# A matmul with scale and add on one core: five hand-written engine programs with their own semaphores in place of a framework's order, and a loop on TensorE

## The chip, the core and the metric

The kernel runs on one core of one Trainium2 chip. The core has five engines that run side by side, each with its own list of instructions: TensorE (PE in the profile; its weight loads are listed as PEld), VectorE (DVE), ScalarE (ACT), GpSimd (POOL) and SyncE (SP), which here only issues transfers. Sixteen DMA engines move data between the chip's memory and the core's on-chip memory. The metric is the time on the device in microseconds (us); smaller is better.

## The reference

```python
batch, m, k, n = 16, 512, 1024, 768
x: (16, 512, 1024) float32     weight: (1024, 768) float32
scale: 0.1                     add_value: (16, 512, 768) float32

return (scale * np.matmul(x, weight) + add_value).astype(np.float32)
```

Taken together the batches give 8192 rows of x. The kernel cuts them into 64 tiles of 128 rows. Each tile is a product of 128 x 1024 by 1024 x 768, and to its result, scaled, 128 x 768 values are added. All in all 33.55 MB of x, 3.15 MB of weight and 25.17 MB of add_value are read, and 25.17 MB are written.

## The kernel before

**Transfers.** `STREAM` lists every transfer in the order in which SP issues them: "x" loads tiles of x, "w" loads slices of the weight, "a" loads add_value and "o" stores results; the two numbers are the first tile (or slice) and how many. All go through one queue. x has room for 16 tiles (`xs`), add_value and the results share 32 tiles' room (`ao`), and the weight lands in the last 8 places of `ao` before it is cast to bf16 (`w_bf`). A load of x waits until the tiles that it overwrites have been read; a store waits until its tiles have been finished; a load of add_value into used room waits until the store from that room has landed. Since SP is in order, what stands behind a waiting transfer waits with it.

**Turning x.** The product needs x with its 1024 inner values on the partitions, so each tile is turned. There are two ways. Tiles 0 to 13 are cast to bf16 (`cast_to`), turned by TensorE in four transposes against an identity matrix (`transpose`, L149), and copied out of PSUM by ACT or DVE (L157). Tiles 14 to 63 go in pairs (`MOVED`): ACT and POOL copy them to bf16 by quadrants of 32 partitions, four copies each for each half of the pair, eight copies each in all (`move_pair`, L110), and DVE turns the pair in one instruction, within 32 x 32 blocks (`turn_moved`, L119). The moved pairs have three buffers (`va`), the turned pairs three (`xt`).

**Products.** For each tile TensorE makes 16 matmuls, eight slices of the inner dimension by two parts of the columns (512 and 256), into one of three PSUM buffers `mm` (`product`, L170). Each weight load is an instruction of its own in the program. DVE then computes scale times the product plus add_value in place in `ao` (`finish`, L178). The first three tiles are multiplied slice by slice as the weight arrives (`head`), scaled into spare room, and their add_value is added later (`added`, L237). The last tile is finished in two parts, 512 columns and then 256.

**Order.** The author writes one sequence of instructions: `STREAM` drives it, `step` does one tile. In `step` the products of tile t come first, then its finish, then the turn of the pair that starts at t+4; the copies for pairs up to six tiles ahead stand in the middle of it. The Tile framework splits the sequence by engine and puts in the semaphores. Everything is unrolled: TensorE's program alone has 1024 products, 1024 weight loads and 56 transposes, 2,084 instructions with its waits.

Of the kernel before, what the change touches and what calls it, by code (L numbers as in the profile page):

```python
# [8 lines left out]

STREAM = [
    ("x", 0, 3), ("w", 0, 2), ("w", 2, 2), ("x", 3, 1), ("w", 4, 4), ("a", 0, 8),
    ("x", 4, 4), ("x", 8, 8), ("a", 8, 8), ("x", 16, 8), ("a", 16, 8), ("x", 24, 8),
# [5 lines left out]
X_SLOTS = 16  # L20
A_SLOTS = 32
XB_BUFS = 3
AHEAD = 4
EARLY = 3

MOVED = [14, 16, 18, 20, 22, 24, 26, 28, 30, 32, 34, 36, 38, 40, 42, 44, 46, 48, 50, 52, 54, 56, 58, 60, 62]
# [3 lines left out]
def kernel(  # L32
# [9 lines left out]
    P = 128  # L42
# [9 lines left out]

    KC = K // (2 * P)
    KJ = 2 * KC
    CUT = 512
    G = 8
# [3 lines left out]
    out_v = out_f.rearrange("(g p t) n -> p g t n", p=P, t=G)  # L60

    def rows(view, s, n):
# [3 lines left out]

    w_v = weight.rearrange("(c p r) n -> p c (r n)", p=P, r=2)

    const = ctx.enter_context(tc.tile_pool(name="const", bufs=1))
    xb_pool = ctx.enter_context(tc.tile_pool(name="xb_pool", bufs=XB_BUFS))  # L70
    xt_pool = ctx.enter_context(tc.tile_pool(name="xt_pool", bufs=3))
    va_pool = ctx.enter_context(tc.tile_pool(name="va_pool", bufs=3))
    tp_pool = ctx.enter_context(
        tc.tile_pool(name="tp_pool", bufs=2, space=bass.MemoryType.PSUM))
    mm_pool = ctx.enter_context(
        tc.tile_pool(name="mm_pool", bufs=3, space=bass.MemoryType.PSUM))
    ctx.enter_context(tc.manual_schedule())

    identity = const.tile([P, P], fp32, name="identity")
    make_identity(nc, identity)  # L80
    xs = const.tile([P, X_SLOTS, K], fp32, name="xs")
    ao = const.tile([P, A_SLOTS, N], fp32, name="ao")
    w_bf = const.tile([P, KJ, N], bf16, name="w_bf")

    xb_tiles, xt_tiles, mm_tiles, done = {}, {}, {}, {"cast": 0, "step": 0, "x": 0}
    in_pair = {t0 + i: t0 for t0 in MOVED for i in range(2)}
    moved, cast_pairs = {}, set()

    def load_w(j, n):

        s = A_SLOTS - KJ + j
        assert j % 2 == n % 2 == 0
        nc.sync.dma_start(  # L93
            ao[:, s:s + n, :].rearrange("p (c r) n -> p c (r n)", r=2),
            w_v[:, j // 2:(j + n) // 2, :])
        for i in range(n):
            nc.vector.tensor_copy(w_bf[:, j + i, :], ao[:, s + i, :])  # L97

    def move_pair(t0, half):


        if half == 0:
            va = va_pool.tile([P, 2 * KC, 4, 64], bf16, tag="va")
            moved[t0] = va
        k = t0 % X_SLOTS
        assert k + 1 < X_SLOTS
        src = xs[:, k:k + 2, :].rearrange("p i (c b k) -> p (i c) b k", b=4, k=64)
        for b in range(4):
            for a, move in ((2 * half, nc.scalar.copy), (2 * half + 1, nc.gpsimd.tensor_copy)):
                move(moved[t0][32 * b:32 * b + 32, :, a, :],  # L110
                     src[32 * a:32 * a + 32, :, b, :])
        if half == 1:
            cast_pairs.add(t0)

    def turn_moved(t0):
        xt = xt_pool.tile([P, 2, KC, P], fp32, tag="xt")
        for i in range(2):
            xt_tiles[t0 + i] = xt[:, i, :, :]
        nc.vector.transpose(  # L119
            xt.rearrange("p i c m -> p (i c m)"),  # L120
            moved.pop(t0).bitcast(fp32).rearrange("p c a k -> p (c a k)"))

    def cast_to(t):
        while done["cast"] <= t:
            i = done["cast"]
            if i in in_pair:
                assert in_pair[i] in cast_pairs
                done["cast"] += 1
                continue
            if len(xb_tiles) == XB_BUFS:  # L130
                break
# [168 lines left out]
```

## Time and profile before

The median of three runs was 210.06 us (209.99 to 210.46). The profiled execution spans 208.4 us from its first to its last instruction; a timed run has some 1.6 us more around that.

| what | busy, us (share) | instructions |
|---|---|---|
| 16 DMA engines, data, mean share | 97.9% | 4448 packets, 87.03 MB |
| PE | 177.1 (85%) | 1059 |
| POOL | 135.2 (65%) | 219 |
| ACT | 129.9 (62%) | 210 |
| DVE | 104.1 (50%) | 113 |
| profiled execution: span | 208.4 | 2843 |

The share of a DMA engine is the time that its packets took. A row of a group of instructions gives the source line, the engine, the operation, what it writes and reads, the shape, the count, the busy time and the mean of one in nanoseconds. "PEclk" is the granted TensorE clock, 1.00 being full speed. The DMA engines fetch the engines' instructions as well; those packets stand in queues of their own, marked "instruction".

### The profile page before, as it was taken

The page shows a single profiled execution, that of the slowest core. Times are in us where ns is not written, and L with a number is a line of the kernel's source. Part 1 is how long each engine was busy: PE and PEld are TensorE (multiplying, and loading weights), DVE is VectorE, ACT ScalarE, POOL GpSimd, SP SyncE. Part 2 cuts the span into 40 slices and gives each one's busy share as a digit, 9 for nine tenths or more (in the row PEclk, how much of TensorE's full clock was granted, in tenths as well). Part 3 has the DMA queues.
Part 4 walks back from the last instruction along what each step waited for, and adds up shares of the span by engine and source line. Part 5 has one row for each costly group of instructions (what it writes and reads, how often), then busy time and mean ns, then how long its engine had stood idle before and what let it go on. Part 6 is the DMA issues. An engine that isn't in the chain of part 4 may idle for free.

```text
span 208.4 us, 2843 instructions
## 1 busy us (share of the span) xinstructions
PE 177.1 (85%) x1059; PEld 108.4 (52%) x1080; DVE 104.1 (50%) x113; ACT 129.9 (62%) x210; POOL 135.2 (65%) x219
## 2 busy tenths in 40 slices
PE   0498339999999999999999999999959996799930
PEld 0355125666666666666666666666626563456510
DVE  0514713555675555566666645475054651555620
ACT  2421100540299999997999559992899919996000
POOL 1310051428699999999999759993899939997000
PEclk9999958999999999999999999999999999999995
DMA  6999999999999999999999999999999999999994
GB/s 229 413 440 448 420 459 406 440 453 415 402 464 434 413 415 425 458 415 428 415 439 451 407 436 425 450 428 407 439 426 437 453 404 426 434 437 425 423 414 187
DMA packets 4461, 87.21 MB, mean 418 GB/s; under 512 B 480, under 2 KB 480, under 8 KB 1120
## 3 DMA queue, kind: packets, MB, share of 16 engines
q1 hardware_dynamic: 4448, 87.03, 97.9%
q8 instruction: 8, 0.13, 0.2%
q14 instruction: 5, 0.04, 0.0%
HBM read 61.87 MB, written 25.17 MB: 418 GB/s over the span
## 4 chain that ended last, share of the span: by engine, by line
DMA 44%; PE 38%; POOL 10%; SPq 1%; issue 1%; DVE 1%; POOLq 0%; DVEq 0%
PE mm L170 36%; DMA out_dram<-ao 17%; DMA ao<-in_add_value_dram 15%; DMA xs<-in_x_dram 12%; POOL va L110 9%; PE tp L149 2%; DVE ao L178 1%; SPq L93 1%; SPq L250 1%; POOL xb L139 1%; SPq L256 0%; POOLq L139 0%; DVEq L178 0%
## 5 line engine op out<-in xcount | busy, mean ns | idle before, releaser
L170 PE MATMUL mm<-w_bf,xt 128*128 128x512 bf16 (+1 forms) x1003 | 170.6, 327 | 8.3 <-DVE ao L178 6.0
L110 ACT CAST va<-xs 32x512 bf16<-32x512 f32 x200 | 123.2, 616 | 46.0 <-DMA xs<-in_x_dram 43.5
L170 PEld LDWEIGHTS <-xt 128*128 128x128 bf16 x1024 | 101.0, 99 | 74.8 <-issue 5.5
L110 POOL CAST va<-xs 32x512 bf16<-32x512 f32 x200 | 121.7, 608 | 20.8 <-DMA xs<-in_x_dram 11.9
L178 DVE SCALAR_TENSOR_TENSOR ao<-mm,ao 128x768 f32<-128x768 f32 (+2 forms) x62 | 57.2, 935 | 40.3 <-PE mm L170 34.0
L119 DVE STREAM_TRANSPOSE xt<-va 128x1024 f32<-128x1024 f32 x25 | 31.1, 1244 | 29.5 <-POOL va L110 29.0
L139 POOL CAST xb<-xs 128x1024 bf16<-128x1024 f32 x11 | 11.2, 1043 | 29.4 <-DMA xs<-in_x_dram 21.8
L149 PE MATMUL tp<-identity,xb 128*128 128x128 f32 x56 | 10.2, 317 | 14.5 <-DVE xb L135 7.7
L149 PEld LDWEIGHTS tp<-identity,xb 128*128 128x128 f32 x56 | 7.7, 163 | 16.4 <-issue 7.7
L157 DVE COPY xt<-tp 128x1024 bf16<-128x1024 bf16 x10 | 6.9, 688 | 10.8 <-PE tp L149 10.8
L157 ACT COPY xt<-tp 128x512 bf16<-128x512 bf16 (+1 forms) x7 | 4.1, 655 | 9.2 <-PE tp L149 9.2
L97 DVE CAST w_bf<-ao 128x768 bf16<-128x768 f32 x8 | 4.0, 555 | 4.9 <-DMA ao<-in_weight_dram 4.9
L135 DVE CAST xb<-xs 128x512 bf16<-128x512 f32 x3 | 1.9, 695 | 7.1 <-DMA xs<-in_x_dram 7.1
L137 POOL CAST xb<-xs 128x512 bf16<-128x512 f32 x2 | 1.6, 835 | 5.9 <-DMA xs<-in_x_dram 5.9
L137 ACT CAST xb<-xs 128x512 bf16<-128x512 f32 x1 | 0.6, 619 | 5.1 <-DMA xs<-in_x_dram 5.1
L237 DVE TENSOR_TENSOR ao<-ao 128x768 f32<-128x768 f32 x3 | 2.7, 953 | 1.1 <-DMA ao<-in_add_value_dram 1.1
L206 DVE TENSOR_SCALAR ao<-mm 128x768 f32<-128x768 f32 x2 | 1.8, 953 | 2.5 <-PE mm L170 2.5
L137 ACT ACT_TABLE_LOAD x1 | 1.3, 1283 | 0.7 <-PEq L281 0.7
L203 ACT ACTIVATE ao<-mm 128x768 f32<-128x768 f32 x1 | 0.8, 817 | 0.0
masks.py:197 POOL MEMSET identity<- 128x128 f32 x1 | 0.2, 205 | 0.3 <-POOLq L281 0.3
masks.py:199 POOL TENSOR_SCALAR_AFFINE_SELECT identity<-identity 128x128 f32<-128x128 f32 x1 | 0.3, 293 | 0.1
L281 POOL MEMSET const-float32-0.0<- 128x1 f32 x1 | 0.1, 98 | 0.2 <-issue 0.2
(3 smaller groups left out, 0.3 us busy)
## 6 DMA issues: line engine op xcount, KB each, us to landing
xs<-in_x_dram SPq DMA_DIRECT2D x7, 4096.0 KB, 23.9
ao<-in_add_value_dram SPq DMA_DIRECT2D x8, 3072.0 KB, 31.1
out_dram<-ao SPq DMA_DIRECT2D x7, 3072.0 KB, 31.3
xs<-in_x_dram SPq DMA_DIRECT2D x1, 2048.0 KB, 24.4
out_dram<-ao SPq DMA_DIRECT2D x1, 1920.0 KB, 9.9
xs<-in_x_dram SPq DMA_DIRECT2D x1, 1536.0 KB, 6.4
ao<-in_weight_dram SPq DMA_DIRECT2D x2, 768.0 KB, 8.5
ao<-in_weight_dram SPq DMA_DIRECT2D x1, 1536.0 KB, 13.2
```

What stands on the lines that cost most here:

```text
L93: nc.sync.dma_start(ao[:, s:s + n, :].rearrange("p (c r) n -> p c (r n)", r=2), w_v[:, j // 2:(j + n) // 2, :])
L97: nc.vector.tensor_copy(w_bf[:, j + i, :], ao[:, s + i, :])
L110: move(moved[t0][32 * b:32 * b + 32, :, a, :], src[32 * a:32 * a + 32, :, b, :])
L119: nc.vector.transpose(xt.rearrange("p i c m -> p (i c m)"), moved.pop(t0).bitcast(fp32).rearrange("p c a k -> p (c a k)"))
L137: other(xb[:, K // 2:K], src[:, K // 2:K])
L139: nc.gpsimd.tensor_copy(xb, src)
L149: nc.tensor.transpose(tp[:, c, :], pairs[:, c * P:(c + 1) * P], identity)
L157: evacuate(xt_tiles[t][:, c:c + q, :].bitcast(bf16), tp[:, c:c + q, :].bitcast(bf16))
L170: nc.tensor.matmul(mm_tiles[t, cols[0]][:, n0:n1], lhs(t, j), w_bf[:, j, n0:n1], start=(j == 0), stop=(j == KJ - 1))
L178: nc.vector.scalar_tensor_tensor(a, mm_tiles[t, part][:, n0:n1], float(scale), a, op0=mybir.AluOpType.mult, op1=mybir.AluOpType.add)
L237: nc.vector.tensor_add(ao[:, t, :], ao[:, EARLY_AT + t, :], ao[:, t, :])
L250: nc.sync.dma_start(xs[:, k:k + n, :], rows(x_v, s, n))
```

## The change

The framework no longer orders the work. Inside one critical section each engine gets a program of its own, written as a function, with semaphores that the kernel allocates: one for each transfer (`landed`), and `by_act`, `by_pool`, `turned`, `casts`, `done` and `made` as counters.

- All tiles are moved by quadrants and turned by DVE; the transposes on TensorE, their identity, the casts and the copies out of PSUM are gone, and so is the special head. Tiles 0 to 7 and 56 to 63 are moved in pairs, tiles 8 to 55 four at once: each copy then has 32 x 1024 elements instead of 32 x 512, and eight copies by each engine serve four tiles. DVE still turns two tiles by one instruction.
- ACT does quadrants 0 and 2, POOL 1 and 3, of the whole group.
- There are two `va` buffers of four tiles, instead of three of two; two pairs of `xt` instead of three; four `mm` buffers instead of three.
- DVE's order is finish(t), finish(t+1), then the turn of the pair that starts at t+4 (t even).
- TensorE runs a loop, 16 times over four tiles. Its waits compare semaphores with a register that the loop advances; its program has 64 matmul instructions, with the weight load implied in each.
- The last tile is finished in one instruction.
- The first transfers are x of two tiles, four slices of weight, x of two tiles, four slices, x of four tiles, then add_value; 29 transfers instead of 30, with the same bytes.

```diff
-    ("x", 0, 3), ("w", 0, 2), ("w", 2, 2), ("x", 3, 1), ("w", 4, 4), ("a", 0, 8),
-    ("x", 4, 4), ("x", 8, 8), ("a", 8, 8), ("x", 16, 8), ("a", 16, 8), ("x", 24, 8),
+    ("x", 0, 2), ("w", 0, 4), ("x", 2, 2), ("w", 4, 4), ("x", 4, 4), ("a", 0, 8),
+    ("x", 8, 8), ("a", 8, 8), ("x", 16, 8), ("a", 16, 8), ("x", 24, 8),
...
-XB_BUFS = 3
-AHEAD = 4
-EARLY = 3
-MOVED = [14, 16, 18, 20, 22, 24, 26, 28, 30, 32, 34, 36, 38, 40, 42, 44, 46, 48, 50, 52, 54, 56, 58, 60, 62]
+MM_BUFS = 4
+XT_PAIRS = 2
+VA_BUFS = 2
+MOVES = [(t, 2) for t in range(0, 8, 2)] + [(t, 4) for t in range(8, 56, 4)] + [
+    (t, 2) for t in range(56, 64, 2)]
...
-    identity = const.tile([P, P], fp32, name="identity")
-    make_identity(nc, identity)
...
+    va = [const.tile([P, 4 * KC, 4, 64], bf16, name=f"va{i}") for i in range(VA_BUFS)]
+    xt = const.tile([P, 2 * XT_PAIRS, KC, P], fp32, name="xt")
+    mm = [psum.tile([P, 1024], fp32, name=f"mm{i}") for i in range(MM_BUFS)]
+
+    landed = {key: tc.alloc_semaphore(f"dma{i}") for i, key in enumerate(STREAM)}
+    by_act, by_pool, turned, casts, done, made = (
+        tc.alloc_semaphore(name)
+        for name in ("by_act", "by_pool", "turned", "casts", "done", "made"))
+
+    def moves_until(t):
+        return 8 * sum(1 for s, _ in MOVES if s <= t)
+
+    def sync_engine(eng):
+        for key in STREAM:
+            op, s, n = key
+            last = s + n - 1
...
+            elif op == "x":
+                if last >= X_SLOTS:
+                    eng.wait_ge(by_act, moves_until(last - X_SLOTS))
+                    eng.wait_ge(by_pool, moves_until(last - X_SLOTS))
+                k = s % X_SLOTS
+                move = eng.dma_start(xs[:, k:k + n, :], rows(x_v, s, n))
+            elif op == "a":
...
+                if s < A_SLOTS <= last + KJ:
+                    eng.wait_ge(casts, KJ)
+                if s >= A_SLOTS:
+                    for key2 in STREAM:
+                        if key2[0] == "o" and key2[1] < last + 1 - A_SLOTS and key2[1] + key2[2] > s - A_SLOTS:
+                            eng.wait_ge(landed[key2], 16)
+                move = eng.dma_start(ao[:, k:k + n, :], rows(add_v, s, n))
             else:
...
+                eng.wait_ge(made, MM_BUFS + last + 1)
+                move = eng.dma_start(rows(out_v, s, n), ao[:, k:k + n, :])
+            move.then_inc(landed[key], 16)
...
+    def mover(eng, copy, parity, count):
...
+        for n, (t, size) in enumerate(MOVES):
+            buf = n % VA_BUFS
+            key = transfer("x", t + size - 1)
+            if key not in seen:
+                eng.wait_ge(landed[key], 16)
+                seen.add(key)
+            if used[buf] is not None:
+                eng.wait_ge(turned, used[buf] + size_of[used[buf]])
+            used[buf] = t
+            k = t % X_SLOTS
+            src = xs[:, k:k + size, :].rearrange("p i (c b k) -> p (i c) b k", b=4, k=64)
+            for a in (parity, parity + 2):
+                for b in range(4):
+                    copy(va[buf][32 * b:32 * b + 32, 0:size * KC, a, :],
+                         src[32 * a:32 * a + 32, :, b, :]).then_inc(count, 1)
...
+    def vector_engine(eng):
...
+        def turn(t):
+            n = next(i for i, (s, size) in enumerate(MOVES) if s <= t < s + size)
+            s, size = MOVES[n]
+            if t == s:
+                eng.wait_ge(by_act, 8 * (n + 1))
+                eng.wait_ge(by_pool, 8 * (n + 1))
+            if t >= 2 * XT_PAIRS:
+                eng.wait_ge(done, t - 2 * XT_PAIRS + 2)
...
+        def finish(t):
...
+            eng.wait_ge(done, t + 1)
+            a = ao[:, t % A_SLOTS, :]
+            eng.scalar_tensor_tensor(
+                a, mm[t % MM_BUFS][:, 0:N], float(scale), a,
+                op0=mybir.AluOpType.mult, op1=mybir.AluOpType.add).then_inc(made, 1)
+
+        eng.sem_inc(made, MM_BUFS)
+        cast_w(0, 4)
+        turn(0)
+        cast_w(4, 4)
+        turn(2)
+        for t in range(T):
+            finish(t)
+            if t % 2 and t + 3 < T:
+                turn(t + 3)
+
+    def tensor_engine(eng):
+        eng.wait_ge(casts, 4)
+        with eng.Fori(1, T + 1, 4) as i:
+            for q in range(4):
+                t = q
+                if q % 2 == 0:
+                    eng.wait_ge(turned, i + (q + 1))
                 for j in range(KJ):
+                    if q == 0 and j == 4:
+                        eng.wait_ge(casts, KJ)
+                    if j == 0:
+                        eng.wait_ge(made, i + q if q else i)
+                    x2 = xt[:, q, j // 2, :].bitcast(bf16).rearrange("p (m r) -> p r m", r=2)
+                    for n0, n1 in ((0, CUT), (CUT, N)):
+                        m = eng.matmul(
+                            mm[q][:, n0:n1], x2[:, j % 2, :], w_bf[:, j, n0:n1],
+                            start=(j == 0), stop=(j == KJ - 1))
+                m.then_inc(done, 1)
+
+    with tc.tile_critical(no_gpsimd_drain=True):
+        sync_engine(nc.sync)
+        mover(nc.scalar, nc.scalar.copy, 0, by_act)
+        mover(nc.gpsimd, nc.gpsimd.tensor_copy, 1, by_pool)
+        vector_engine(nc.vector)
+        tensor_engine(nc.tensor)
```

## The prediction

> **What bounds the kernel now.** I read the slices and the queues of the page first, then the windows, then who waits for whom.
>
> ```profile
> PEclk9999958999999999999999999999999999999995
> DMA  6999999999999999999999999999999999999994
> ...
> q1 hardware_dynamic: 4448, 87.03, 97.9%
> q8 instruction: 8, 0.13, 0.2%
> q14 instruction: 5, 0.04, 0.0%
> ```
>
> The DMA engines are busy in every slice but the first and the last: 97.9% of 208.4 us is 204 us for each of them. No compute engine comes near (PE 177). The windows show the rate and the end:
>
> ```profile
> 60.00:80.00 20.00, 19.90 (x123) 12.03 (x123) 12.28 (x12) 19.57 (x33) 18.63 (x31) 1.00 1.01 431
> ...
> 203.00:204.00 1.00, 0.00 (x0) 0.00 (x0) 0.00 (x0) 0.00 (x0) 0.00 (x0) 0.90 0.96 409
> 204.00:205.00 1.00, 0.00 (x0) 0.00 (x0) 0.00 (x0) 0.00 (x0) 0.00 (x0) 0.50 0.81 341
> 205.00:206.00 1.00, 0.00 (x0) 0.00 (x0) 0.00 (x0) 0.00 (x0) 0.00 (x0) 0.50 0.55 230
> 206.00:207.00 1.00, 0.00 (x0) 0.00 (x0) 0.00 (x0) 0.00 (x0) 0.00 (x0) 0.50 0.15 65
> ```
>
> The last two columns are the DMA share and GB/s. The rate is 430 GB/s throughout, then falls in steps: the sixteen engines do not finish together. Each transfer lands when the slowest is done, so the ragged end costs time. The trace's completion records give its size. For the add_value that lands at 28.1 us the sixteen signals came within 0.7 us; for the last store between 204.6 and 207.5, 2.85 us apart. In between, the spread jumps where an instruction fetch strikes: the packet records of q8 have eight packets of 16 KB, 0.9 to 1.1 us each, at 35.8, 54.8, 73.6, 94.3, 115.6, 135.2, 158.7 and 183.4. After the first, one signal of sixteen is 1.86 us behind the first instead of 0.7, and that engine never catches up, since its queue is always full. Eight 16 KB blocks are 131 KB: TensorE's 2,084 unrolled instructions at 64 bytes (133 KB).
>
> So the time is the data's time plus the lag of the unluckiest engine, as long as SP never issues late. Compute need only keep ahead:
>
> ```profile
> SPq L250 <- ACT va L110: 63.7, 5, 19.5
> SPq L264 <- DVE ao L178: 41.8, 4, 22.5
> SPq L256 <- DMA out_dram<-ao: 34.0, 4, 9.6
> ```
>
> SP waits often, but the queue still holds transfers meanwhile.
>
> **The change part by part.** Bytes are unchanged (87.03 MB). At 430 GB/s a tile of x takes 1.22 us, a tile of add_value, of results or a slice of weight 0.915. I follow the first due times. An issue takes about 1.0 us to its first packet (0.74 to 1.76 at the start).
>
> ```profile
> L110 ACT CAST va<-xs 32x512 bf16<-32x512 f32 x200 | 123.2, 616 | 46.0 <-DMA xs<-in_x_dram 43.5
> L110 POOL CAST va<-xs 32x512 bf16<-32x512 f32 x200 | 121.7, 608 | 20.8 <-DMA xs<-in_x_dram 11.9
> ...
> L119 DVE STREAM_TRANSPOSE xt<-va 128x1024 f32<-128x1024 f32 x25 | 31.1, 1244 | 29.5 <-POOL va L110 29.0
> L139 POOL CAST xb<-xs 128x1024 bf16<-128x1024 f32 x11 | 11.2, 1043 | 29.4 <-DMA xs<-in_x_dram 21.8
> ```
>
> *Moves.* A copy of 512 elements takes 0.61 us; of 1024 no row exists on 32 partitions. Bounds: 0.61 (nothing for length) and 1.22 (twice). The nearest row, POOL's 128 x 1024 cast, says 1.04; I take it, and 0.04 between copies. A pair takes 8 x 0.65 = 5.2 us, four tiles 8.7. All moves: POOL 64 x 0.61 + 96 x 1.04 = 139 us (busy 135 before), ACT the same (130 before).
>
> *PE.* It loses 56 transposes: 0.44 us for four, 6.2 in all. Finishes in the middle of the run come every 2.60 us, so 64 tiles are 166 us. *DVE:* 64 x 0.95 + 32 x 1.25 + 8 x 0.5 = 105 us (104 before): it trades 10 copies of 0.69, the head's scaling and additions for 7 turns.
>
> *Head.* Tiles 4 to 7 land at about 20.5 (17.1 us of transfers after 1.8, some 0.5 of slow start and 0.9 of lag); their two pairs are moved by 31.1. That frees x 16 to 23, issued at 32.3 before. Due: the transfers ahead of it last to 44, so by 43. Meanwhile turn(4) stands on DVE behind finish(0), which waits for add_value at 27.8, so tile 4 starts at 31.0. Tiles 8 to 15 land at 37.6, the first four are moved by 46.3, the next by 55.0. That releases x 24 to 31 (54.6 before); due at 60, 5 us of slack. Tile 8 can start at 47.5, and at half clock (16 matmuls took 4.18 instead of 2.60 at 30.3), so PE stands 3.3 us behind before, whose finish(8) began at 48.4. That costs nothing yet: unbroken, PE would be through at 47.5 + 1.6 + 56 x 2.60 = 194.7.
>
> *End.* With four `mm` buffers tile 60, not 59, is first to need the finish of 56, whose add_value lands last (185.6 before; I take 184, as the lag shrinks). turn(60) stands behind finish(56) and finish(57): 187.1; four tiles, 10.4: 197.5; one finish of 0.95 (not 0.69 and 0.42 with the first part beside PE): the last store issues at 198.5, or at 200.1 if add_value still lands at 185.6. Before issued at 200.3. It must come by 200.8: the fastest engine's 2.74 us of it ended at 204.6, less 1.0. So nothing starves, and the price of all this is nothing, hidden by the queue.
>
> *Fewer fetches.* TensorE's program shrinks to some 140 instructions, so q8's eight packets should go. Worth at least their mean share, 8.3/16 = 0.5 us; at most 2.1, the final spread falling from 2.85 to the early 0.72. Twelve of the sixteen signals end 1.1 us or more after the first and only eight packets were removed, so some lag stays: short fetches on q14 and slow packets where loads and stores mix. I take 1.4.
>
> *The loop.* Sixteen back edges with register steps. The trace has no branch of this kind. The row for cover is the drain that closes PE's program:
>
> ```profile
> L295 PEldq DRAIN  x2: 13/1564/3115, 196.8 to 208.0; - x2
> ```
>
> The sequencer reached it at 196.8 and it lasted 3.1 us, to PE's last product: the sequencer runs 3.1 us ahead of the array. A back edge below that is hidden while PE is fed; above it, each microsecond costs PE one, sixteen times. In the middle the loop's top also waits for turn(t), which ends some 3 us before tile t starts. Bounds: nothing, and 3.1 us times 14; I take nothing, by that row.
> The Trainium skill, "Runtime: NRT & Kernel Launch", Instruction fetch mechanics, speaks against the change twice. It calls the crossing of a 16 KiB block mostly hidden, by which the fetches were free and the sum 0.4 above before; the completion records show them hidden from PE but not from the DMA engine that carries them. And it says that a taken branch outside the two-page window stalls for a fetch; here the body is smaller than a block, and no row shows such a branch. By that rule, if the window were missed, there would be sixteen fetches for eight and the saving would turn into a loss.
>
> *Weight loads.* They are implied in the matmuls now. The transposes already stood so, and four in a row took 0.44 us: loads overlapped. Nothing.
>
> *Entry and exit.* The critical section adds a hop at each end. The two rounds that end the kernel take 0.64 us (207.72 to 208.36). I take 0.1 more at the start, 0.3 at the end; bounds 0 and 0.8 together.
>
> **Sum.** 208.4 - 1.4 + 0.4 = 207.4 us of span. The median stands 1.66 above the profiled span: 209.1. Bounds: 210.06 - 2.1 + 0 = 208.0, and 210.06 - 0.5 + 0.8 = 210.4.
>
> **Rivals.** A difference under 0.2% (0.42 us) can't be told from none here; the three runs spread over 0.47.
>
> *Exposed back edge (slower).* Place: the loop's end, from tile 8 on, fourteen times, with PE never idle. PE's end must stay below 199.8 (200.8 less finish and issue); unbroken it is 194.7, so an exposed edge over 5.1/14 = 0.36 us decides. At 0.6 us PE ends at 203.1, the last store lands 3.3 later than the queue allows: 212.4. For it: the start at 47.5 has eaten PE's reserve. Against: the 3.1 us of lead.
>
> *Long moves (slower).* One mover group that lasts 16 copies m (with gaps) after 37.6 must be done by 60: m up to 1.40. At 1.5 the first starved transfer is x 24, 1.6 us: 210.7; more follows at the two-buffer `va`, since the next group needs its turn. Against: the 1.04 row.
>
> *The saving fails (same).* Other lags, or loop refetches, replace the eight packets: 210.06 + 0.4 = 210.4; with the saving at its floor, 209.9.
>
> **How the numbers follow.** Forecast case 0.64, saving fails 0.16, back edge 0.11, long moves or another late transfer 0.09. The likeliest gives 209.1, its own range 208.0 to 210.0. Leaving out a little at the low end and the dearer half of the slower cases, the range is 208.2 to 211.2. Faster by over 0.2%: the forecast but for its upper edge, and the saving's floor now and then: 0.63. Within: 0.16. Slower: 0.21.
>
> **What would show it.** Right: q8 gone or at one packet; the DMA share of the last microseconds falling within about 1.5 us instead of 3; DMA at 9 in all inner slices; x 24 to 31 issued near 55; PE's waits at tile 60 on a turn; four-tile copies near 1040 ns. Wrong: q8 at 16 or more; a slice of DMA below 9; PE at full share to its end with issue gaps every four tiles; SP's last store after 201; an end longer than 1.3 us after the last landing.

## The result, and the profile after

The changed kernel is slower. Its median is 211.52 us (210.52 to 211.91, six runs) against 210.17 us (209.98 to 210.5) for the kernel before on the same chip: a ratio of 1.0053, 95% interval 1.0036 to 1.0071. A second set of eight runs gave 211.04 against 210.41, 1.0042 (1.0026 to 1.0057). The forecast was 209.1 and "faster", with a range of 208.2 to 211.2; 211.52 lies above the range, the second set's 211.04 just inside.

Single executions differ more than before's do: 210.5 to 212.05 over the fourteen, with a standard deviation of 0.5 us against 0.27 for the 95 runs of the kernel before that were made beside the experiments. So means over runs are compared below, not one profile with another: 211.27 for the changed kernel, 210.41 for the kernel before, +0.86 us.

The page of the changed kernel: granted clock and DMA share in 40 slices, then the queues with packets, megabytes and share of time.

```profile
PEclk9999997996999999999999999999997999999995
DMA  6999899999999999998999999999999999999991
...
q1 hardware_dynamic: 4432, 87.03, 97.2%
q14 instruction: 3, 0.02, 0.0%
```

The queue of TensorE's fetches, q8, is gone, as forecast, and DMA is at 8 or 9 in every inner slice. Yet the data's share fell from 97.9% of 208.4 us to 97.2% of 210.0: both are 204 us of work for each DMA engine, in a longer span. The windows near the end (the last two columns are the DMA share and GB/s):

```profile
60.00:80.00 20.00, 19.89 (x123) 11.99 (x124) 12.27 (x12) 18.73 (x19) 18.92 (x19) 1.00 1.00 426
200.00:203.00 3.00, 0.42 (x3) 0.03 (x1) 0.96 (x1) 0.00 (x0) 0.00 (x0) 1.00 0.82 347
203.00:204.00 1.00, 0.00 (x0) 0.00 (x0) 0.00 (x0) 0.00 (x0) 0.00 (x0) 1.00 0.97 402
204.00:205.00 1.00, 0.00 (x0) 0.00 (x0) 0.00 (x0) 0.00 (x0) 0.00 (x0) 0.86 1.07 449
205.00:206.00 1.00, 0.00 (x0) 0.00 (x0) 0.00 (x0) 0.00 (x0) 0.00 (x0) 0.50 0.23 92
206.00:207.00 1.00, 0.00 (x0) 0.00 (x0) 0.00 (x0) 0.00 (x0) 0.00 (x0) 0.50 0.22 92
207.00:208.00 1.00, 0.00 (x0) 0.00 (x0) 0.00 (x0) 0.00 (x0) 0.00 (x0) 0.50 0.13 55
```

The end is cleaner and as long. Between 200 and 203 us the share is down to 0.82, because the last store is issued so late (201.44) that the early engines run out of work. Before, the share sank in steps of a few engines. Now twelve of sixteen engines finish within 0.2 us of each other, at 205.4, and then almost nothing moves for three microseconds: 92 GB/s, then 55. Four engines are late, two of them by 3.0 us. The completion records of the last store say the same:

```
last store, sixteen signals:   first    last    spread   mean
before                         204.61   207.46   2.85    206.03
after                          205.42   208.40   2.99    206.10
```

Until 54 us the sixteen signals of the changed kernel agree within 0.35 us; the fetches that struck before are indeed not there. At 54.9 two fetches of 8 KB, on q14, put two engines some 0.8 us behind the first. Then the spread grows, and not at fetches: 1.22 us at 78.8, 1.61 at 95.8, 2.29 at 120, 2.54 at 144, 3.54 at 183. These are moments at which the stream passes from a load to a store.

Compute did most of what was forecast. The groups of instructions by shape, with the busy time, the mean of one in nanoseconds and the idle time before them:

```profile
L131 ACT CAST va<-xs 32x1024 bf16<-32x1024 f32 x96 | 100.1, 1043 | 32.8 <-DMA xs<-in_x_dram 27.9 <-DVE xt L154 2.7
L131 POOL CAST va<-xs 32x1024 bf16<-32x1024 f32 x96 | 99.3, 1034 | 33.6 <-DMA xs<-in_x_dram 26.5 <-DVE xt L154 1.6
...
L131 POOL CAST va<-xs 32x512 bf16<-32x512 f32 x64 | 40.0, 624 | 19.1 <-DMA xs<-in_x_dram 15.5
L154 DVE STREAM_TRANSPOSE xt<-va 128x1024 f32<-128x1024 f32 x32 | 39.5, 1235 | 21.2 <-POOL va L131 19.9 <-ACT va L131 1.3
```

A copy of 1024 elements takes 1.04 us, not 0.61 and not 1.22. x 24 to 31 was issued at 55.3 (forecast 55.0). TensorE's only wait after 140 us is for the turn of tile 48:

```profile
PE mm L194 <- DVE xt L154: 3.3, 1, 3.3
```

From 48 us to that wait, and from its end at 157.0 to 200.42, it has no gap above 0.5 us, across all back edges of its loop. The last store is issued at 201.44.

The edges of the program, from the profile's records of single instructions: the first transfer is issued at 0.94 us instead of 0.74, and from the last landing to the end it takes 1.57 us instead of 0.97. Of these 0.60 us, some 0.43 pass before SP reaches the closing rounds of signals, with the hops out of the critical section, and 0.17 is one instruction of GpSimd that clears a range of semaphores: 0.265 us instead of 0.096.

### The profile page after: what moved, and what is told of

The parts are those of the page before. It is cut to its first block, busy times and chain, and to the rows that moved or that the text cites. A ratio compares the mean times of both kernels' runs of the same rounds, so it can differ in the third digit from the quotient of the medians.

```text
span 210.0 us, 2723 instructions
## 1 busy us (share of the span) xinstructions
PE 172.3 (82%) x1008; PEld 101.7 (48%) x1024; DVE 103.2 (49%) x104; ACT 140.8 (67%) x161; POOL 139.5 (66%) x164
## 3 DMA queue, kind: packets, MB, share of 16 engines
q1 hardware_dynamic: 4432, 87.03, 97.2%
## 4 chain that ended last, share of the span: by engine, by line
DMA 43%; POOL 28%; PE 21%; issue 2%; SPq 1%; DVE 1%; DVEq 0%
DMA xs<-in_x_dram 43%; POOL va L131 28%; PE mm L194 21%; SPq L95 1%; DVE xt L154 1%; SPq L89 0%; DVE ao L166 0%; SPq L104 0%; DVEq L151 0%; SPq L93 0%; SPq L235 0%; DVEq L149 0%; SPq L199 0%
## 5 line engine op out<-in xcount | busy, mean ns | idle before, releaser
L194 PE MATMUL mm<-w_bf,xt 128*128 128x256 bf16 (+1 forms) x1008 | 172.3, 332 | 28.1 <-DVE xt L154 24.7
L131 POOL CAST va<-xs 32x1024 bf16<-32x1024 f32 (+1 forms) x160 | 139.3, 870 | 52.7 <-DMA xs<-in_x_dram 42.0
L131 ACT CAST va<-xs 32x1024 bf16<-32x1024 f32 (+1 forms) x160 | 139.5, 872 | 49.8 <-DMA xs<-in_x_dram 43.5
L194 PEld LDWEIGHTS mm<-w_bf,xt 128*128 128x128 bf16 x1024 | 101.7, 100 | 98.4 <-DVE xt L154 25.8
L166 DVE SCALAR_TENSOR_TENSOR ao<-mm,ao 128x768 f32<-128x768 f32 x64 | 60.3, 951 | 65.2 <-PE mm L194 52.3
L154 DVE STREAM_TRANSPOSE xt<-va 128x1024 f32<-128x1024 f32 x32 | 39.5, 1235 | 21.2 <-POOL va L131 19.9
L142 DVE CAST w_bf<-ao 128x768 bf16<-128x768 f32 x8 | 6.0, 804 | 11.8 <-DMA ao<-in_weight_dram 11.8
```

The source lines that it names most:

```text
L131: copy(va[buf][32 * b:32 * b + 32, 0:size * KC, a, :], src[32 * a:32 * a + 32, :, b, :]).then_inc(count, 1)
L142: eng.tensor_copy(w_bf[:, j, :], ao[:, A_SLOTS - KJ + j, :]).then_inc(casts, 1)
L154: eng.transpose(xt[:, k:k + 2, :, :].rearrange("p i c m -> p (i c m)"), va[n % VA_BUFS][:, q:q + 2 * KC, :, :].bitcast(fp32).rearrange("p ...
L166: eng.scalar_tensor_tensor(a, mm[t % MM_BUFS][:, 0:N], float(scale), a, op0=mybir.AluOpType.mult, op1=mybir.AluOpType.add).then_inc(made, 1)
L194: m = eng.matmul(mm[q][:, n0:n1], x2[:, j % 2, :], w_bf[:, j, n0:n1], start=(j == 0), stop=(j == KJ - 1))
```

## The experiments

Three explanations stood against each other: A, the forecast's, by which instruction fetches make the slowest engine's lag; B, by which the lag is made where the stream passes from a load to a store (a "passage" below; there are six in either kernel), and fetches only choose whom it strikes; C, by which the loop itself costs time. Two questions were added later: what the critical section costs, and whether the new order of moves, turns and products costs anything.

The table collects all that is compared below. "Landing" is the mean over a kernel's runs of the span less the time from the last landing to the end, that is, when the last byte arrived; "first issue" and "end" come from one trace each, and "end" is the time from the last landing to the end; "outside" is what a timed run has beyond its span.

| kernel | median, us | ratio to before, 95% | first issue | landing | end | outside |
|---|---|---|---|---|---|---|
| before | 210.41 (95 runs) | | 0.74 | 207.7 | 0.97 | 1.79 |
| changed, both sets | 211.52, 211.04 | 1.0053, 1.0042 | 0.94 | 207.9 | 1.57 | 1.77 |
| e1, e12: unrolled | 211.60, 211.44 | 1.0065, 1.0053 | 0.94 | 208.2 | 1.57 | 1.79 |
| e3: stores grouped | 210.73 | 1.0016 (1.0006-1.0026) | 0.94 | 207.4 | 1.57 | 1.79 |
| e13: grouped, unrolled | 210.63 | 1.0013 (1.0004-1.0021) | 0.94 | 207.3 | 1.57 | 1.79 |
| e2, e16: loads for stores | 209.4, 209.51 | 0.9957 (0.9943-0.9972) | 0.94 | 206.1 | 1.57 | 1.79 |
| e15: the same, unrolled | 210.37 | 0.9992 (0.9979-1.0006) | 0.94 | 207.0 | 1.57 | 1.80 |
| e19: tiles 48 on in pairs | 211.21 | 1.0042 (1.0027-1.0058) | 0.94 | 207.5 | 1.94 | 1.79 |
| e9: before with a section | 211.44 | 1.0049 (1.0035-1.0064) | 0.74 | 207.6 | 1.89 | 2.03 |
| e17: changed order, no section | 211.09 | 1.0042 (1.0029-1.0055) | 0.73 | 207.8 | 1.03 | 2.34 |
| e18: the same, grouped | 210.33 | 1.0002 (0.9991-1.0012) | 0.73 | 206.9 | 1.03 | 2.40 |

### The loop undone

```diff
-        with eng.Fori(1, T + 1, 4) as i:
-            for q in range(4):
-                t = q
+        for t in range(T):
+            q = t % 4
...
```

> The changed kernel with TensorE's loop written out again (1024 matmuls, waits against constants), nothing else altered. Theory A, the prediction's: every 16 KB fetch puts about 1.2 us of lag on one DMA engine for good, and the loop saved eight of them; the queue with eight 16 KB packets comes back and the time rises by 0.5 to 1.4 us, to 212.0 to 212.9. Theory B: the lag of the slowest engine is made at the points where the queue passes from loads to stores, and the fetches only choose whom it strikes; the eight packets come back, but the last store still lands 2.5 to 3.6 us after its first signal and the time stays within 0.5 us of 211.5. Theory C: the loop itself costs; the time falls below 211.

> The changed kernel once more, beside the next two on the same chip, for a second trace of the lag. All theories: 211.2 to 211.8; the spread of the last signals 2.5 to 3.6 us if the passages set it.

> TensorE's loop written out once more, on the same chip as the run with the loop, to narrow the loop's worth. By the prediction 1.4 us slower than the loop (bounds 0.5 to 2.1); by the first pair of runs 0.1, with an uncertainty of some 0.5.

With TensorE's program unrolled the eight fetches are back (its page):

```profile
q8 instruction: 8, 0.13, 0.2%
q14 instruction: 3, 0.02, 0.0%
```

The time hardly notices the loop: 211.60 against 211.52, and in the second pair 211.44 against 211.04. By means over 11 and 14 runs the loop saves 0.28 us, 95% interval about 0 to 0.6. C falls: a program without the loop is not faster. A, with 1.4 us, falls as well: the spread of the last store was 3.02 and 3.07 us with the fetches, 2.99 and 2.22 without. (The last, from e11, is below the 2.5 that was expected, as its 211.04 is below 211.2.)

The mean engine does notice. For the store before the last, the mean of the sixteen signals comes at 202.94 and 202.86 us with the loop, at 203.68 and 203.58 unrolled: 0.73 us sooner. That is what the fetches cost by the packet records: eight packets of 0.98 us, each with some 0.43 us lost beside it, are 11.3 us over sixteen engines, 0.7 each. But the time waits for the slowest signal, and that comes at 205.66 and 204.47 with the loop, at 205.17 and 205.65 without.

### The stores taken away

```diff
-                move = eng.dma_start(rows(out_v, s, n), ao[:, k:k + n, :])
+                if last < 56:
+                    move = eng.dma_start(ao[:, k:k + n, :], rows(add_v, s, n))
+                else:
+                    move = eng.dma_start(rows(out_v, s, n), ao[:, k:k + n, :])
```

> The changed kernel with the seven stores of tiles 0 to 55 replaced by loads of the same number of bytes into the same room (so those results are left out), all waits as they are. Theory A: fetches alone make the lag, so the sixteen signals of a late transfer still come 2.5 us apart or more. Theory B: with no passage from loads to stores before the last two transfers, the spread stays where the two fetches at 55 us put it, under 1.3 us, and the last store lands 1 to 2 us earlier than 208.4.

> The loop with loads in place of the seven stores once more (those results are left out), beside the unrolled one on the same chip: spread about 1 us, 209.2 to 209.6.

> TensorE written out, and loads of the same bytes in place of the seven stores of tiles 0 to 55 (those results are left out). If a 16 KB fetch lags its DMA engine by 1.2 us for good, as the prediction had it, the spread at the end is 1.6 to 2.6 us and the time 0.7 to 1.6 us above the loop with the same loads. If fetches cost nothing at the end even so: spread under 1.2 us, times equal within 0.3.

The same bytes go through the same queue at the same places, but up to tile 55 as loads, so the results of these tiles are not written. With the loop the sixteen signals stay 0.95 to 0.97 us apart from 86 us to the end, and the time falls to 209.5. The windows near the end of e2 and, below, of e15, the same kernel unrolled:

```profile
204.00:205.00 1.00, 0.00 (x0) 0.00 (x0) 0.00 (x0) 0.00 (x0) 0.00 (x0) 0.50 0.68 286
205.00:206.00 1.00, 0.00 (x0) 0.00 (x0) 0.00 (x0) 0.00 (x0) 0.00 (x0) 0.50 0.07 28
206.00:207.00 1.00, 0.00 (x0) 0.00 (x0) 0.00 (x0) 0.00 (x0) 0.00 (x0) 0.50 0.00 0
```

```profile
205.00:206.00 1.00, 0.00 (x0) 0.00 (x0) 0.00 (x0) 0.00 (x0) 0.00 (x0) 0.50 0.59 249
206.00:207.00 1.00, 0.00 (x0) 0.00 (x0) 0.00 (x0) 0.00 (x0) 0.00 (x0) 0.50 0.09 37
```

At 205 us the first has 28 GB/s left, the second 249; its spread is 2.02 us instead of 0.97. That is the forecast's mechanism by itself: the eight fetches cost 0.86 us (209.51 against 210.37, where the runs of each lie within 0.25). It is real, and it has the size that the forecast bounded (0.5 to 2.1). But it shows only in a kernel that hardly stores. With stores the last byte arrives 1.8 us later with the loop, 1.2 us later without, and little of the difference between the two is left. In e2 the last store is also issued 2.5 us sooner (198.94), but this is not what the stores cost: in the changed kernel the last signal of the last store comes 2.74 us after that of the store before, as in e2 (2.73), so the slowest engine did not wait for the issue.

The packet records say where the time goes. Counted are packets of 24 or 32 KB that took over 0.2 us longer than the median of their size (0.91 and 1.21 us). "At a passage" means from 1.7 us before the first signal of a load that a store follows to its last signal; "at a fetch" means within 1.6 us before or 2.0 after one. The pair of numbers is how many, and their extra time in us.

```
                            fetches  passages   at a fetch   both      at a passage   all
before                         13       6        10 / 4.6    7 / 2.3     4 / 1.0     21 /  7.9
changed                         3       6         3 / 1.2    0          21 / 9.2     24 / 10.4
changed, second set             3       6         3 / 1.1    0          14 / 4.5     20 /  6.4
e1   unrolled                  11       6        11 / 4.8    0          19 / 7.4     31 / 12.6
e12  unrolled                  11       6        12 / 5.0    0          21 / 6.1     38 / 13.1
e3   grouped                    3       3         3 / 1.5    0           5 / 1.7      8 /  3.2
e13  grouped, unrolled         11       3        10 / 4.7    8 / 2.8     2 / 0.9     20 /  8.3
e16  loads for stores           3       -         3 / 1.6    0           0            3 /  1.6
e15  the same, unrolled        11       -        11 / 5.5    0           0           11 /  5.5
```

A fetch costs the engine that carries it 0.4 to 0.5 us beside its own packet, in every version. The loop took that away, some 4 us over all engines. Where there are stores, three to nine microseconds more are lost at six passages: the slow packets there, most of them the last of the load, take 1.1 to 1.85 us. Without stores there is not one slow packet away from a fetch. This is B, and it is shown as far as it goes. The two traces of the changed kernel point the same way: with 9.2 us lost at passages the last byte arrived at 208.40, with 4.5 at 207.22. The loss is not a fixed price, though: at the same six passages the kernel before lost 1.0 us (3.3 with the packets that are at a fetch too). Why a load's last packets slow down while other engines begin to store, and why more in one execution than in another, was not settled.

### Fewer passages, and more

Stores in groups of two, three passages instead of six:

```diff
-    ("x", 8, 8), ("a", 8, 8), ("x", 16, 8), ("a", 16, 8), ("x", 24, 8),
-    ("a", 24, 8), ("o", 0, 8), ("x", 32, 8), ("o", 8, 8), ("a", 32, 8), ("x", 40, 8),
-    ("o", 16, 8), ("a", 40, 8), ("x", 48, 8), ("o", 24, 8), ("a", 48, 8), ("x", 56, 8),
-    ("o", 32, 8), ("a", 56, 8), ("o", 40, 8), ("o", 48, 8), ("o", 56, 5), ("o", 61, 3),
+    ("x", 8, 8), ("a", 8, 8), ("x", 16, 8), ("a", 16, 8), ("x", 24, 8), ("a", 24, 8),
+    ("x", 32, 8), ("o", 0, 8), ("o", 8, 8), ("a", 32, 8), ("x", 40, 8), ("a", 40, 8),
+    ("x", 48, 8), ("o", 16, 8), ("o", 24, 8), ("a", 48, 8), ("x", 56, 8), ("a", 56, 8),
+    ("o", 32, 8), ("o", 40, 8), ("o", 48, 8), ("o", 56, 5), ("o", 61, 3),
```

> The changed kernel with the stores grouped by two in the list of transfers, so that the queue passes from loads to stores three times instead of six; the same transfers, waits and bytes. Theory A: the lag comes from fetches, as many as before, so the time stays at 211.5 give or take 0.4. Theory B: the spread of the last signals falls from 3.0 to about 1.5 to 2 us and the time falls by 1 to 1.5 us, to 210.0 to 210.5.

> The grouped stores (three passages) with TensorE written out, the fourth corner beside the loop, the unrolled loop and the grouped loop (210.73). If fetches matter where the passages don't drown them: 0.5 to 1.2 us slower than the grouped loop, 211.2 to 211.9. If they don't matter at all: 210.7 give or take 0.3.

Grouping takes 0.6 to 0.9 us off the landing (207.9 to 207.4 with the loop, 208.2 to 207.3 without). B had expected more of the loop version, 210.0 to 210.5 with a spread of 1.5 to 2 us; it took 210.73 and the spread was 2.28. With the stores grouped the loop is worth nothing: 210.73 with it, 210.63 without. The window of e3 at 205 us has 55 GB/s where the changed kernel had 92:

```profile
205.00:206.00 1.00, 0.00 (x0) 0.00 (x0) 0.00 (x0) 0.00 (x0) 0.00 (x0) 0.50 0.13 55
206.00:207.00 1.00, 0.00 (x0) 0.00 (x0) 0.00 (x0) 0.00 (x0) 0.00 (x0) 0.50 0.04 18
```

The same was tried three times on the kernel before: e6 with the grouping as above, e10 with o 0 and o 8 ahead of x 32, e14 with o 16 and o 24 ahead of x 48 as well.

> The kernel before, its own engine order and all its fetches, with the stores grouped by two in the list of transfers as in the grouped run of the changed kernel (three passages from loads to stores instead of six). Theory B: the lag belongs to the passages, in this kernel as in the other, so the last signals come about 2 us apart instead of 2.85 and the time falls by 0.5 to 1 us, to 209.3 to 209.8. Theory A, fetches: no change, 210.2 to 210.4. If the engine order needs the old places of the transfers, it gets slower.

> The kernel before with its stores grouped by two again, but the first two stores put ahead of x 32 to 39, so that no load of x is asked for before its room is free (in the first grouped run of this kernel x 32 came 1.5 us late). Three passages from loads to stores. Theory B: the last signals come 2 to 2.5 us apart instead of 2.85, the last landing about 1 us earlier, 209.2 to 209.9 on the scale where before is 210.4. Theory A: no change. The rival on this kernel: x 32 lands 7 us later than before and TensorE falls behind by more than its 6 us of idle time; then slower than before.

> The kernel before with the stores in three groups, each group where the next load of x can be asked for in time (x 32 is due at 92, x 48 at 141, and both were issued by 126 in the run before). Theory B: spread 2 to 2.5 us, last landing at 206.4 to 206.9, time 0.4 to 1.0 us below before. Theory A: no change. The rival: x 48 lands at 151 instead of 146, TensorE ends later than 200 and the time rises.

They took 210.95, 211.93 and 211.79 us (ratios 1.0023, 1.0076, 1.0068) and answer nothing, since in each a transfer was issued too late. In e6 x 32 went out with 1.3 us of work left in the queue and landed 1.5 us late; in e10 the same befell x 48. In e14 the last two stores went out 1.2 and 0.5 us after the first engine had run out of work. Its page, in the last three slices:

```profile
DMA  6999999999999999999999999999999999999785
```

Then pieces of four tiles instead of eight, once taking turns (e7, eleven passages), once two and two (e8, six):

```diff
+    ("o", 0, 4), ("x", 32, 4), ("o", 4, 4), ("x", 36, 4), ("o", 8, 4), ("a", 32, 4), ("o", 12, 4), ("a", 36, 4),
... e8:
+    ("o", 0, 4), ("o", 4, 4), ("x", 32, 4), ("x", 36, 4), ("o", 8, 4), ("o", 12, 4), ("a", 32, 4), ("a", 36, 4),
```

> The changed kernel with the transfers between tile 24's add_value and tile 40's store cut to four tiles and loads and stores taken in turn: eleven passages from loads to stores instead of six, same bytes. Theory B: the spread at the end is 0.7 to 2 us larger than in the run with the same pieces in the old order, and the time as much longer. Theory A: both runs have the same time within 0.4 us.

> The control: the same pieces of four tiles, the two halves of each old transfer behind each other, so six passages as before. Both theories: within 0.5 us of the changed kernel, 211.1 to 212.0; if smaller pieces or more issues cost by themselves, it shows here.

They took 212.16 and 211.98, 0.18 apart where at least 0.7 was expected. In the traces the last landing is 0.64 us apart (208.74 and 208.10). The smaller pieces cost time by themselves: the packets of the data take 205.7 us (e7) and 205.3 us (e8) of each engine where the changed kernel's take 204.1, so neither run can be compared with that kernel. With packets of 12 and 16 KB counted as well, those over 0.2 us above the median of their size lost 8.1 us at the passages in e7 and 2.0 in e8; with one trace of each, where two traces of the changed kernel differ by 4.7, this is no proof. B in its simple form, so much for each passage, misses: from six to eleven almost nothing is added, and the spread is at most 3.61 us in any trace. An engine that is already behind seems not to be struck again as others are; that was only argued.

### The last store sooner or later

```diff
-MOVES = [(t, 2) for t in range(0, 8, 2)] + [(t, 4) for t in range(8, 56, 4)] + [
-    (t, 2) for t in range(56, 64, 2)]
+MOVES = [(0, 2), (2, 2)] + [(t, 4) for t in range(4, 64, 4)]
... e19:
+MOVES = [(t, 2) for t in range(0, 8, 2)] + [(t, 4) for t in range(8, 48, 4)] + [
+    (t, 2) for t in range(48, 64, 2)]
```

> The changed kernel with tiles 4 to 7 and 56 to 63 moved four at once too, which takes 24 instructions from ACT's and POOL's programs. If the two fetches at 55 us (ACT's and POOL's, 8 KB each) vanish and they are the seed of the lag (theory A), the spread at the end falls under 1.3 us and the time by 1 to 2 us. If they stay, or theory B holds, the time stays at 211.5 give or take 0.5. The tail itself may gain a little: four tiles take 8.3 us to move instead of 10.2 for two pairs.

> The changed kernel with tiles 48 to 55 moved in pairs as well (fours only for 8 to 47). In its trace TensorE waits 3.3 us for the four tiles at 48, goes on at half clock and runs unbroken to 200.42, so that the last store is issued at 201.44, when the fast engines have 0.6 us of work left. Moved in pairs, tile 48 starts some 3.5 us sooner, TensorE ends near 197 and the last store is issued near 198. If the time is set by the slowest engine's lag alone, whose queue holds data until 205.7: no change beyond 0.2 us, 211.0 to 211.5. If the late last store, or the lag that it shares with the three passages of the grouped kernels (issue at 200.45 and 199.59), is what made the order dear: 0.4 to 0.8 less, 210.5 to 210.8.

With fours to the end (e5) TensorE waits 3.3 us at tile 56, runs at a lower clock for a while (0.66 granted between 180 and 190 us) and ends at 204.87. The windows show the work stopping and starting again:

```profile
203.00:206.00 3.00, 1.87 (x12) 0.95 (x10) 1.22 (x2) 0.00 (x0) 0.00 (x0) 1.00 0.16 67
206.00:208.00 2.00, 0.00 (x0) 0.00 (x0) 0.00 (x0) 0.00 (x0) 0.00 (x0) 0.86 0.70 295
```

67 GB/s between 203 and 206: the last store, issued at 205.89, finds all queues empty, and its signals come within 0.19 us. It took 212.67 (1.0111, 1.0095 to 1.0126). By the two traces, a last store issued 4.45 us later landed 1.66 us later (210.06 against 208.40); the lag of the slowest engine had covered the rest.

With pairs from 48 on (e19) the store was issued at 200.52, not near 198: TensorE now waited for tile 56. By the mean over its runs the last byte arrived at 207.5, 0.4 us sooner than in the changed kernel (with an uncertainty of 0.2), but the time is 211.21. In this build the end takes 1.94 us instead of 1.57: GpSimd's hop there takes 0.39 us instead of 0.08, from 208.33 on, and two 8 KB fetches on q14 start at 209.42 and 209.80, around the end of the span at 209.55. That the fetches cause the slow hop is not shown; their packets start after it.

The times alone do not decide, but the traces do. In the kernel before, the changed kernel, e1, e12, e3, e13, e17, e18 and e19 the last signal of the last store comes 2.71 to 2.75 us after the last signal of the store before, the time of three tiles, whether the last store was issued at 199.59 (e18) or at 201.44: the slowest engine went from one to the other without a pause. So an earlier issue of the last store does not bring the last byte sooner in these versions, and the gain of the grouping (e3 issued at 200.45) is not that. What e19 has less of is loss at passages, 3.6 us in its one trace.

### The critical section, and the order without it

An empty critical section, put into the kernel before, after its last store:

```diff
...
+    manual.close()
+    gate = tc.alloc_semaphore("gate")
+    with tc.tile_critical(no_gpsimd_drain=True):
+        nc.sync.sem_inc(gate, 1)
+        for eng in (nc.scalar, nc.gpsimd, nc.vector, nc.tensor):
+            eng.wait_ge(gate, 1)
```

> The kernel before with a critical section in which nothing is done but one signal from SP to the other engines, entered after the last store has landed: it adds the entry and the exit of such a section to the path and nothing else. From the rows of the changed kernel (first issue 0.94 instead of 0.74, end 1.58 instead of 0.96 after the last landing) 0.6 to 1.0 us, so 210.9 to 211.3 on the scale where before is 210.3. The rival, that the hops cost next to nothing and the changed kernel's whole loss lies in the transfers: within 0.3 us of before.

It cost 0.98 us. The landing is not later (207.6 against 207.7); the end is 1.89 us instead of 0.97, and 0.24 us more lie outside the span. Nothing hides what stands behind the last landing. The run says nothing of the section's start.

And the reverse, the changed kernel's transfers, moves, turns and buffers written as one sequence that the framework splits, with tiles of pools and no semaphores of its own:

```diff
-    with tc.tile_critical(no_gpsimd_drain=True):
-        sync_engine(nc.sync)
-        mover(nc.scalar, nc.scalar.copy, 0, by_act)
-        mover(nc.gpsimd, nc.gpsimd.tensor_copy, 1, by_pool)
-        vector_engine(nc.vector)
-        tensor_engine(nc.tensor)
+    ctx.enter_context(tc.manual_schedule())
...
+    for op, s, n in STREAM:
...
+        elif op == "x":
+            while last >= X_SLOTS and done["group"] <= group_of[last - X_SLOTS]:
+                step()
```

> The changed kernel's transfers, moves, turns, buffers and order of each engine, but written as one sequence again that the framework splits: no critical section, no semaphores of the kernel's own, and so TensorE unrolled. If the critical section is what the changed kernel pays (0.2 us at the start and 0.6 at the end in its trace, 0.98 when an empty one was added to the kernel before): 0.8 to 1.0 below the unrolled changed kernel (211.6 and 211.44), so 210.5 to 210.7, within 0.2% of the kernel before, with the end 0.97 us after the last landing and a spread near 3. If the order of moves, turns and products itself costs the time: about 211.4, with the end 0.97 us after a last landing near 208.4.

> The same with the stores grouped by two (three passages from loads to stores instead of six). The grouped changed kernel took 210.73 with the loop and 210.63 unrolled. If the section's cost and the passages' are separate terms: 0.8 to 1.0 below that, 209.6 to 209.9, 0.2 to 0.4% below the kernel before, with a spread of 2.3 to 2.7. If the order itself costs the time: 210.4 or more.

By the time alone the order would be guilty: 211.09. The parts say otherwise. The first transfer is issued at 0.73 and the last landing is followed by 1.03 us, about as in the kernel before. This also prices the section's start: of the same list of transfers, the one that lands at 28 us has its mean signal at 27.54 and 27.51 here (e17, e18), at 27.72 to 27.78 in the changed kernel and its unrolled and grouped forms, so the 0.2 us are still there. The last byte arrives at 207.8, 0.1 us later than before, with all fetches and all six passages:

```profile
q8 instruction: 8, 0.13, 0.2%
q14 instruction: 3, 0.02, 0.0%
```

The time is lost outside the span: 2.34 us there in the mean, 2.2 to 2.5 in every run, where all other kernels have 1.8 (e9 2.03). In the traces of these two, and of no other kernel, an 8 KB fetch on q14 starts 1.0 us after the span's end (209.86 and 209.32). That it is the cause is likely, but a build in which it falls elsewhere was not tried, and e9 has its 0.24 us more without such a fetch. Grouped, the order lands at 206.9, 0.7 us before the kernel before, and still takes the same time, 210.33 against 210.25, where 209.6 to 209.9 was expected. No version that computes everything beat the kernel before.

## Why the prediction was wrong

**The step that failed** is "Fewer fetches", with "I take 1.4". Its first half was right to the packet: the eight packets of q8 vanished, and the engines ran within 0.35 us of each other until 54 us. Its second half, that the lag at the end shrinks by as much, was wrong. Measured against the same kernel unrolled the saving is 0.28 us (0 to 0.6), and nothing where the stores are grouped. The text named "slow packets where loads and stores mix" as a reason why some lag stays. They are the main source: 4.5 to 9.2 us of packet time in the changed kernel, against 1.1 to 1.2 at its fetches. The mean share that the forecast took as its floor was there (0.73 us by the signals); it went to the mean engine, and the time goes by the slowest. The kernel before was read as if every jump of the spread were a fetch; seven of its 21 slow packets lie at a fetch and at a passage alike, and four at a passage alone. Nor does its spread jump at each fetch: it goes from 0.71 to 1.86 us at the first, is still at 1.88 after the next two, and reaches 2.85 over the other five and the six passages. Two smaller readings were off as well: the transfer that lands at 28.1 us is x 4 to 7, not add_value, and TensorE's 2,084 instructions are fewer than the products, weight loads and transposes that are said to be in them (2,104).

The Trainium skill, "Runtime: NRT & Kernel Launch", Instruction fetch mechanics, calls the crossing of a block "mostly hidden". The forecast set the records of the carrying engine above that rule. In the time of this kernel the rule came nearer (0.28 of a possible 2.1 us); without the stores it did not hold (0.86 us). Its warning of branches met nothing here: no fetch of TensorE appears in the looped kernel.

**The second term** is "Entry and exit": 0.1 and 0.3 were taken, with 0.8 as the bound of both. Measured are 0.20 and 0.60, the bound itself. The empty section (0.98 us) shows that the part at the end goes into the time in full; the part at the start is still there at 28 us, and whether all of it reaches the last landing is not shown. The forecast counted rounds and overlooked that the kernel's own semaphores are cleared at the end (0.17 us).

**The sum with measured terms**, over means: 210.41 - 0.28 + 0.20 + 0.60 = 210.93. The order by itself lands 0.1 later (e17). Some 0.25 remain to 211.27; they lie in the landing of the versions with the critical section, and what makes them stays open.

**Right, by the traces:** *Moves* 1.04 us; *PE* 2.60 us a tile; *The loop* and *Weight loads* nothing (unrolled is not faster, and TensorE has no gap above 0.5 us from 157.0 to 200.4); *Head* within 0.5 us for the start of tile 8 (47.97) and the issue of x 24 (55.3).

**Wrong without a price: *End*.** The chain through the add_value of tile 56 and the turn of tile 60 did not bind. Tile 48 did: x 48 landed at 146.8, its four tiles were moved in 8.5 us, and TensorE lost 3.3 us and then some clock (0.92 granted between 140 and 160 us). The forecast followed this for tiles 8 and 60 alone. The last store was issued at 201.44, past the limit of 200.8 that it had set. That, after 201, and an end of more than 1.3 us (1.57) were among the signs of being wrong that it had named. The twelve early engines went without work for about 0.6 us, but the last engine still had work up to 205.66, and the three tiles' 2.74 us after that give its 208.40: the late issue cost no time.

**The rivals.** The case that came true is *The saving fails*, given 0.16 at 210.4; its price lacked the other half of entry and exit (210.06 + 0.8 = 210.9). *Exposed back edge* and *Long moves* did not occur.

## What to carry to other kernels

Before a lag's removal is booked, look for what else makes it, and whether that is there already under the first cause: here the spread of the last transfer is remade where loads turn into stores, and a version that hardly stored showed the fetches' price (0.86 us) where the whole kernel showed 0.28. A program in a critical section with semaphores of its own paid at both ends here, 0.20 and 0.60 us, and the part behind the last landing was hidden by nothing. A lag that is spread over sixteen engines has a mean and a slowest; price a change by the slowest. In a kernel bound by transfers, split the time into first issue, landing, end and what lies outside the span, over several runs, before a difference below 1 us is given a cause.

## What the runs showed of the hardware

- As a load ended and the next store began, packets took up to 1.85 us instead of 1.21 (32 KB, which are loads of x) and up to 1.79 instead of 0.91 (24 KB) in the first trace of the changed kernel; without stores there was no such packet.
- The spread between the sixteen engines was at most 3.61 us (e12), with six passages or eleven, with three fetches or eleven.
- An instruction fetch of 16 KB took 0.9 to 1.1 us of its DMA engine and 0.4 to 0.5 us more from the data packet beside it; eight of them made the mean engine 0.73 us later.
- The clearing of semaphores at the end took 0.096 us (kernel before), 0.138 (with the empty section) and 0.265 us (with 35 semaphores of the kernel's own).
- In the build with 8 KB instruction fetches 0.13 us before and 0.26 us after the end of the span, the end was 0.37 us longer (1.94 against 1.57); the two builds with such a fetch 1.0 us after the span had 0.5 to 0.6 us more outside it. That the fetches are the cause is not shown.
